# Low parts of the turned probabilities on GpSimd, and the neighbourhood's row tiles turned by VectorE through DRAM

## The chip, the cores and the metric

The kernel runs on one core of a Trainium2 chip. The metric is the device time of one execution in microseconds (us); the median of three runs is taken. The engines are named as the profile names them: PE (TensorE's matmuls), PEld (its weight loads), DVE (VectorE), ACT (ScalarE), POOL (GpSimd) and SP (SyncE, which issues nearly all DMAs).

## The reference

The kernel computes two layers of a hybrid attention block on 16 meta tokens and 512 grid tokens (64 by 8), in float32, and a final normalisation. Of each layer:

```python
h = rms_norm(x, norm_g)
qa, ka, va, za, qb, kb, vb, zb, ga, gb = split_cols(einsum('bld,de->ble', h, w_in))
qa, ka = (apply_axial_rope(rms_norm(t, g), cos, sin) for t, g in ((qa, q_norm_g), (ka, k_norm_g)))
oa = gqa_attention(qa, ka, va) * silu(za)                 # 8 query heads, 2 key heads, all 528 keys
ob = neighbourhood_attention(qb, kb, vb, rpb) * silu(zb)  # 8 heads, a clamped window of 8 x 16 keys, plus the meta keys
mixed = sigmoid(ga) * (oa @ w_o_attn) + sigmoid(gb) * (ob @ w_o_na)
x = x + mixed @ w_out
```

Both attentions are a softmax of scores (the second with a learned bias by relative place) times the values. `gqa_attention` is called the global branch here, `neighbourhood_attention` the neighbourhood.

## The kernel before

Activations lie with features on the partitions and tokens along the row. Every large matmul is made of three: a float32 operand is split into a high part (rounded to the matmul's type, a cast on ACT) and a low part (the rest, a subtraction), and high by high, high by low and low by high are added in PSUM.

**Weights.** A product (`product`, `project`) multiplies a chunk of 128 weight columns by all tokens. Its weights come in two halves of 128x512: a DMA brings `raw`, ACT casts it to `whi` (L240), POOL subtracts to get `wlo` (L241), PE uses both (L325 to L327). `raw`, `whi` and `wlo` have 4 buffers each, and halves are asked for 3 ahead. In the first layer a product runs over two spans of 264 tokens (2 x 24 matmuls), each in one of two PSUM banks; in the second most run over one span of 512. `y` names the products with the two output matrices, which use one half each.

**The two branches** run beside the products. After each span `tick()` is called (in the second layer also in the middle of a span), and `GQA_AT` and `NA_AT` say at which tick after its start a piece of work makes each step. A new unit of the global branch (one head, 256 queries; 16 a layer) and a new head of the neighbourhood (8 a layer) start every fourth tick at most.

A unit of the global branch (`global_unit`): `scores` (PE `S`, DVE maximum L837, ACT exponential L841, giving `P`), `turn` (DVE transposes 32x32 blocks in place, L867, and a DMA writes the tile to DRAM), `back` (four DMAs read it so that blocks land in their turned places, L877), `split_part` (ACT casts `pth`, L193; DVE subtracts `ptl`, L194), `split_ends` (the same for the meta keys, `ga`, L896 and L898) and `sums` (PE `av`, L905). `combine` then copies half of the result on ACT (`cmb`, L769) and adds it on DVE.

A head of the neighbourhood (`windowed_head`): `prepare` loads a bias tile of 128x960, `scores` (PE `Sb`, DVE L990, ACT exponential L992, in place in the bias tile), then nine 128-row transposes on PE into PSUM banks `ta`, `tb`, `tc` (L129) in three steps, each followed by a split from PSUM (`tah`/`tal`, `tbh`/`tbl`, `na`), and `sums` (PE `avb`, L1052), collected at the end of the tick by `combine`. In the first layer there is one more transpose, `tm`, for the meta queries.

**What sets the order.** A scheduler lays the recorded instructions out into one fixed row for each engine. Program order is its guide, `high_priority` (as in `split`) moves instructions ahead, and it also moves instructions of other work forward where it reckons that an engine would stand idle. On the chip each engine goes through its row strictly in order, and waits on semaphores. SP does the same with the DMAs.

Of the kernel before, what the change touches and what calls it, by code (L numbers as in the profile page):

```python
# [11 lines left out]
F32 = mybir.dt.float32  # L12
# [24 lines left out]
GQA_AT = ({"scores": (0, 1), "turn": (1, 2), "back": 3, "split": (5, 5), "ends": 5, "divide": (3, 4, 6), "sums": (7, 7)},  # L37
          {"scores": (0, 1), "turn": (1, 2), "back": 3, "split": (5, 5), "ends": 5, "divide": (3, 4, 6), "sums": (7, 7)})
NA_AT = ({"stages": (0, 2, 5, 5, 5, 7), "values": (3, 4), "divide": (3, 4, 6)},
         {"stages": (0, 2, 4, 5, 5, 7), "values": (3, 4), "divide": (3, 4, 6)})  # L40
# [55 lines left out]
def trunk_kernel(ctx: ExitStack, tc: tile.TileContext, xT, w, gn, gf, bias, rope, out):  # L96
# [94 lines left out]
    def split(hi, lo, src):  # L191
        with tc.high_priority():
            split_at["hi"] = nc.scalar.copy(hi, src)  # L193
            split_at["any"] = nc.vector.tensor_sub(lo, src, hi.bitcast(F32))  # L194
# [259 lines left out]
    for l in range(DEPTH):  # L454
# [310 lines left out]
        def combine(tag, o, hh, av, c0, n):  # L765
# [4 lines left out]
            with ExitStack() as held:  # L770
                if "max" in newest:
                    held.enter_context(tc.issue_after(newest["max"].ins))
                nc.vector.tensor_add(o[r, c0:c0 + n], av[r, :n], t[r, :n])
# [73 lines left out]
        def global_unit(kv, parts, n, name, done):  # L847
# [35 lines left out]
            def split_part(kt):  # L883
                v = c["both"][:, :width * 4].rearrange("p (x k i) -> p x k i", k=4, i=32)[:, :, kt:kt + per]
                th, tl = slot("G", f"pth{name}_{kt}", F32R), slot("G", f"ptl{name}_{kt}", F32R)
                split(*(t[:, :width * per].rearrange("p (k x i) -> p x k i", k=per, i=32) for t in (th, tl)), v)
# [4 lines left out]
            def split_ends():  # L891

                tm, m = pad_tile("ga"), c["meta"][:, :n]
                with tc.high_priority():
                    for t in range(len(parts)):
                        nc.scalar.copy(tm[32 * t:32 * t + 32, n * t:n * (t + 1)], m)  # L896
                    for t in range(len(parts)):
                        nc.vector.tensor_sub(tm[64 + 32 * t:96 + 32 * t, n * t:n * (t + 1)], m, tm[:32, :n].bitcast(F32))  # L898
# [67 lines left out]

        def windowed_head(hd):
# [39 lines left out]
            def transposes1():  # L1007
                pb = c["p"]
                tp = bank(ps_t, f"ta{nm}", "tp")
                for i, (b, o0) in enumerate(((0, 80), (1, 16), (1, 144), (2, 0))):  # L1010
                    transposed(tp[:, P * i:P * (i + 1)], pb[b][:, o0:o0 + P])
                c["a"] = slot("B", f"tah{nm}", F32R), slot("B", f"tal{nm}", F32R)
                split(c["a"][0][:, :512], c["a"][1][:, :512], tp)
                if full:
                    ps = bank(ps_t, f"tm{nm}", "tp")[:32]
                    transposed(ps[:, :P], c["pm"])
                    ps = ps[:, :NMETA]
                    mh = pad_tile("mm")
                    nc.vector.tensor_copy(mh[:32], ps)
                    nc.vector.tensor_sub(mh[64:96], ps, mh[:32].bitcast(F32))  # L1020
                    c["mt"] = mh

            def transposes2():
                pb = c["p"]
                tp = bank(ps_t, f"tb{nm}", "tp")
                transposed(tp[:, 0:P], pb[2][:, P:2 * P])
                transposed(tp[:, P:2 * P], pb[3][:, 0:P])
                transposed(tp[:EDGE, 2 * P:3 * P], pb[0][:, :EDGE])
                transposed(tp[:EDGE, 3 * P:4 * P], pb[3][:, P:P + EDGE])
                c["b"] = bh, bl = slot("B", f"tbh{nm}", F32R), slot("B", f"tbl{nm}", F32R)  # L1030
                split(bh[:, :256], bl[:, :256], tp[:, :256])
                split(bh[:EDGE, 256:512], bl[:EDGE, 256:512], tp[:EDGE, 256:512])

            def transposes3():
                tp = bank(ps_t, f"tc{nm}", "tp")
                transposed(tp[:64, :P], c["bias"][:, BLK_META:BLK_META + 64])

                c["m"] = tm = pad_tile("na")
                split_meta([(tm[:, P:2 * P], tp[:, :P]), (tm[:, :P], tp[:, :P])], inner)

            def sums():
                VB2, o = kvq[j]["v2"], kvq[j]["o"]
                av = bank(ps_a, f"avb{nm}", "avn")
                seq = [(5, c["m"], 0, 128, 384)]
                for t in c["a"]:
                    seq += [(0, t, 0, 0, 256), (1, t, 256, 128, 384)]
# [268 lines left out]
```

## Time and profile before

| | us |
|---|---|
| three runs: median (lowest, highest) | 853.73 (852.26, 855.82) |
| the profiled execution, its own time | 855.46 |
| its span, first to last instruction | 853.1 |
| PE busy in it (share) | 825.1 (97%) |
| DVE, ACT, POOL busy | 552.0, 473.7, 382.6 |
| mean granted TensorE clock | 0.992 |

Busy time is the union of an engine's instructions in the profile. A matmul's duration there runs from its start to the end of its results, and the next one starts before that; how long PE takes for one is read from start to start. "Idle before" an instruction is time in which its engine did nothing, and the name behind it is the instruction whose end released it.

### The profile page before, as it was taken

How to read it: one execution, taken by the hardware profiler on the slowest of the kernel's cores; microseconds unless marked ns; L12 is line 12 of the kernel's file. 1: busy time of each engine (PE TensorE's matmuls, PEld its weight loads, DVE VectorE, ACT ScalarE, POOL GpSimd, SP SyncE). 2: the span in 40 equal slices, each digit the busy share in tenths (PEclk: the TensorE clock that was granted, in tenths of full speed). 3: DMA queues.
4: the chain of work that ended last, by engine and by line, in shares of the span. 5: the costliest groups of instructions: out<-in, count | busy, mean ns of one | idle time of the engine just before them, and what ended most of it. 6: DMA issues, size and time to landing. Idle time of an engine off the chain costs nothing.

```text
span 853.1 us, 16107 instructions
## 1 busy us (share of the span) xinstructions
PE 825.1 (97%) x5662; PEld 762.1 (89%) x5662; DVE 552.0 (65%) x1218; ACT 473.7 (56%) x1137; POOL 382.6 (45%) x296
## 2 busy tenths in 40 slices
PE   9999899989999999899999999999999999999997
PEld 9999899989999999899998989898987778878786
DVE  7976658777776675436447657777777657555633
ACT  8654677566764555333435456576757645543422
POOL 1663343343343333545765554443534433445851
PEclk9999999999999999999999999999999999999999
DMA  7277464566544564334555575657476655544502
GB/s 275 90 194 215 122 183 122 172 205 169 169 139 137 164 184 145 112 100 144 147 143 130 142 212 161 170 165 238 124 206 172 193 163 169 169 151 145 176 13 99
DMA packets 113249, 135.00 MB, mean 158 GB/s; under 512 B 31888, under 2 KB 66192, under 8 KB 113168
## 3 DMA queue, kind: packets, MB, share of 16 engines
q1 hardware_dynamic: 112448, 132.90, 53.0%
q8 instruction: 45, 0.74, 0.4%
q10 hardware_dynamic: 720, 1.06, 0.3%
q14 instruction: 36, 0.29, 0.1%
HBM read 98.50 MB, written 21.84 MB: 141 GB/s over the span
## 4 chain that ended last, share of the span: by engine, by line
PE 78%; DVE 8%; ACT 6%; issue 4%; DMA 2%; SPq 1%; POOL 1%; POOLq 0%; ACTq 0%; DVEq 0%
PE pp L327 16%; PE pp L325 16%; PE pp L326 16%; PE av L905 4%; PE y L327 3%; PE y L326 3%; PE y L325 3%; PE avb L1052 2%; DVE ptl L194 2%; PE pf L1234 2%; PE pf L1236 2%; PE pf L1235 2%; PE S L556 2%; PE S L557 1%; DVE ga L898 1%
## 5 line engine op out<-in xcount | busy, mean ns | idle before, releaser
L241 POOL TENSOR_TENSOR wlo<-raw,whi 128x512 fp32r<-128x512 f32 x210 | 289.2, 1386 | 404.7 <-ACT whi L240 325.0
L325 PE MATMUL pp<-hh,whi 128*128 128x264 f32 (+3 forms) x1040 | 326.6, 314 | 2.7 <-DVE mg L1131 1.5
L327 PE MATMUL pp<-hh,wlo 128*128 128x264 f32 (+3 forms) x1040 | 326.2, 314 | 1.3 <-POOL wlo L241 1.2
L326 PE MATMUL pp<-hl,whi 128*128 128x264 f32 (+3 forms) x1040 | 324.3, 312 | 0.0
L327 PEld LDWEIGHTS pp<-hh,wlo 128*128 128x128 f32 x1040 | 196.8, 189 | 12.9 <-POOL wlo L241 2.1
L325 PEld LDWEIGHTS pp<-hh,whi 128*128 128x128 f32 x1040 | 196.5, 189 | 12.4 <-DVE mg L1131 1.7
L326 PEld LDWEIGHTS pp<-hl,whi 128*128 128x128 f32 x1040 | 197.0, 189 | 9.5
L240 ACT CAST whi<-raw 128x512 fp32r<-128x512 f32 x210 | 127.6, 618 | 109.1 <-PE pp L326 41.1
L867 DVE STREAM_TRANSPOSE P<-P 128x512 f32<-128x512 f32 x64 | 46.4, 727 | 36.4 <-ACT P L841 35.7
L194 DVE TENSOR_TENSOR ptl<-P,pth 128x512 fp32r<-128x512 f32 x64 | 53.8, 841 | 5.4 <-ACT pth L193 4.7
L837 DVE CUSTOM_DVE_ANT_1 P<-S,r 128x528 f32<-128x528 f32 x64 | 44.9, 701 | 16.0 <-PE S L557 15.1
L1131 DVE TENSOR_TENSOR mg<-pp,rbc 128x264 f32<-128x264 f32 (+1 forms) x48 | 24.8, 517 | 39.0 <-PE pp L327 38.5
L841 ACT ACTIVATE P<-P,st 128x528 f32<-128x528 f32 x64 | 47.2, 737 | 1.9
L1132 ACT ACTIVATE mg<-mg 128x264 f32<-128x264 f32 (+1 forms) x48 | 23.7, 494 | 35.0 <-DVE mg L1131 34.8
L992 ACT ACTIVATE bias<-bias,stb 128x208 f32<-128x208 f32 (+1 forms) x64 | 31.0, 486 | 20.0 <-DVE stb L990 19.9
L193 ACT CAST pth<-P 128x512 fp32r<-128x512 f32 x64 | 39.3, 614 | 0.1
L840 ACT ACTIVATE st<-st 128x1 f32<-128x1 f32 x64 | 13.0, 203 | 45.4 <-DVE st L837 44.6
L905 PE MATMUL av<-ptl,VA 128*128 128x256 f32 x128 | 34.1, 294 | 3.3 <-DVE ptl L194 3.1
L326 PE MATMUL pp<-mx,whi 128*128 128x264 f32 x128 | 36.6, 286 | 0.0
L327 PE MATMUL pp<-mx,wlo 128*128 128x264 f32 x128 | 36.4, 284 | 0.0
L325 PE MATMUL pp<-mx,whi 128*128 128x264 f32 x128 | 36.3, 284 | 0.0
L905 PE MATMUL av<-pth,VA 128*128 128x256 f32 x128 | 34.8, 295 | 0.0
(534 smaller groups left out, 1731.6 us busy)
## 6 DMA issues: line engine op xcount, KB each, us to landing
raw<-in_w_dram SPq DMA_DIRECT2D x210, 256.0 KB
turn<-P SPq DMA_DIRECT2D x32, 528.0 KB
P<-turn SPq DMA_DIRECT2D x128, 128.0 KB
bias<-in_bias_dram SPq DMA_DIRECT2D x16, 480.0 KB
KB<-KB SPq DMA_DIRECT2D x24, 272.0 KB
rawl<-in_w_dram SPq DMA_DIRECT2D x16, 256.0 KB
x<-in_xT_dram SPq DMA_DIRECT2D x8, 264.0 KB
xr<-in_xT_dram SPq DMA_DIRECT2D x8, 264.0 KB
```

The source lines that it names most:

```text
L193: split_at["hi"] = nc.scalar.copy(hi, src)
L194: split_at["any"] = nc.vector.tensor_sub(lo, src, hi.bitcast(F32))
L240: cast = nc.scalar.copy(hi, raw)
L241: sub = nc.gpsimd.tensor_sub(lo, raw, hi.bitcast(F32))
L325: nc.tensor.matmul(ps, wh, rh[:, a:b], start=i == 0, stop=False)
L326: nc.tensor.matmul(ps, wh, rl[:, a:b], start=False, stop=False)
L327: nc.tensor.matmul(ps, wl, rh[:, a:b], start=False, stop=i == n - 1)
L837: newest["max"] = nc.vector.tensor_tensor_reduce(p[:n].rearrange("p (i k) -> p i k", i=2), S[:n, :, :HALF], scale[:n].unsqueeze(2).to_broa ...
L841: nc.scalar.activation(p[:n], p[:n], AF.Exp, bias=st[:n, 1:2], scale=1.0, accum_out=st[:n, 2:3] if total is None else total)
L867: nc.vector.transpose(c["both"][:n, a:b], c["both"][:n, a:b])
L905: nc.tensor.matmul(c["av"], rows2(c["t"][i][0]), c["t"][i][1], start=i == 0, stop=i == 8)
L992: nc.scalar.activation(pb[b], pb[b], AF.Exp, bias=st[:, b:b + 1], scale=-1.0, accum_out=total[:, b:b + 1])
```

## The change

The diff, cut to its core (names in the code before stand above):

```diff
-GQA_AT = (... "divide": (3, 4, 6) ...          # both layers
+GQA_AT = (... "divide": (2, 3, 5) ...
-NA_AT = ({"stages": (0, 2, 5, 5, 5, 7), ...}, {"stages": (0, 2, 4, 5, 5, 7), ...})
+NA_AT = ({"stages": (0, 2, 3, 4, 4, 4, 6, 7), ...}, {"stages": (0, 2, 3, 4, 4, 6, 7), ...})

-    def split(hi, lo, src):
+    def split(hi, lo, src, eng=nc.vector):
...
-            split_at["any"] = nc.vector.tensor_sub(lo, src, hi.bitcast(F32))
+            split_at["any"] = eng.tensor_sub(lo, src, hi.bitcast(F32))

             def split_part(kt):
...
-                split(*(... for t in (th, tl)), v)
+                split(*(... for t in (th, tl)), v, nc.gpsimd)
             def split_ends():
...
-                        nc.vector.tensor_sub(tm[64 + 32 * t:96 + 32 * t, ...], m, tm[:32, :n].bitcast(F32))
+                        nc.gpsimd.tensor_sub(tm[64 + 32 * t:96 + 32 * t, ...], m, tm[:32, :n].bitcast(F32))

-            def transposes1(): ...   # 4 PE transposes, split of 128x512 from PSUM
-            def transposes2(): ...   # 4 PE transposes, splits of 128x256 and 80x256 from PSUM
-            def transposes3(): ...   # 1 PE transpose, split of the meta keys
+            def turn():
+                v = c["bias"][:, EDGE:EDGE + 832].rearrange("p (s x) -> p s x", s=2)[:, :, :3 * P]
+                for s in range(2):
+                    nc.vector.transpose(v[:, s], v[:, s])
+                c["there"] = dpool.tile([P, 6 * P], F32, tag="turnedb", bufs=3, name=f"turnb{nm}")
+                nc.sync.dma_start(c["there"].rearrange("p (s x) -> p s x", s=2), v)
+            def meta_turn(): ...     # first layer: tm and its split, as before
+            def edges():
+                pb = c["p"]
+                tp = bank(ps_t, f"tb{nm}", "tp")
+                transposed(tp[:EDGE, :P], pb[0][:, :EDGE])
+                transposed(tp[:EDGE, P:2 * P], pb[3][:, P:P + EDGE])
+                transposed(tp[:64, 2 * P:3 * P], c["bias"][:, BLK_META:BLK_META + 64])
+                ...                  # splits of 80x256 and of the meta keys
+            def back():
+                there = c["there"].rearrange("(b j) (s x) -> j s b x", j=32, s=6)
+                for q in range(4):
+                    nc.sync.dma_start(c["bias"][32 * q:32 * q + 32, :6 * P].rearrange("j (s b i) -> j s b i", s=6, b=4),
+                                      there[:, :, :, 32 * q:32 * q + 32])
+            def split_tiles():
+                v = c["bias"][:, :6 * P].rearrange("p (s t x) -> p t s x", s=2, t=3)
+                c["a"] = slot("B", f"tah{nm}", F32R), slot("B", f"tal{nm}", F32R)
+                split(*(... for t in c["a"]), v[:, :2])      # 128x512, from SBUF
+                split(*(... for t in c["b"]), v[:, 2])       # 128x256, from SBUF
```

So three of a head's nine transposes stay on PE (two of 80 columns, one of 64, all in one bank), and the six whole tiles of 128x128 take the way of the global branch: two DVE transposes of 128x384 in place, one DMA out, four DMAs back with pieces of 32 numbers, and a split from SBUF at tick 6. `sums` makes the same eleven matmuls in another order (meta keys, edges, whole tiles), writing the tiles in queries' blocks, and `combine` reads them with the columns rearranged. In the global branch the subtractions `ptl` and `ga` move from DVE to POOL, and the steps that spread the inverse sums come one tick earlier.

How the rows change is shown at two places. In names, the numbers are layer, then chunk or head (and unit), then half, then a serial number: `whi0_16_1` is the cast of the second weight half of chunk 16 in layer 0, `avb0_1` the products of the neighbourhood's head 1.

**First place: layer 0, chunk 16, beside head 1.** On ACT, before:

```order
L240 CAST whi0_16_0_1822<-raw0_16_0_1695 128x512
L240 CAST whi0_16_1_1828<-raw0_16_1_1820 128x512
L193 CAST tah0_1_1789<-ta0_1_1784 128x512
L757 ACTIVATE zb0_1t_1688<-zb0_1_1687 128x264
L193 CAST tbh0_1_1802<-tb0_1_1797 128x256
L792 ACTIVATE na0_122<-tc0_1_1808,inner_130 32x128 x2
L193 CAST tbh0_1_1802<-tb0_1_1797 80x256
```

and now:

```order
L769 COPY cmb1973_1974<-avb0_1_1937 64x512
L769 COPY cmb1977_1978<-avbm0_1_1949 64x16
L996 ACTIVATE bias0_2_1763,sumb0_1_1762<-bias0_2_1763,stb0_2_1861 128x208
L996 ACTIVATE bias0_2_1763,sumb0_1_1762<-bias0_2_1763,stb0_2_1861 128x272 x2
L996 ACTIVATE bias0_2_1763,sumb0_1_1762<-bias0_2_1763,stb0_2_1861 128x208
L240 CAST whi0_16_1_1822<-raw0_16_1_1814 128x512
L240 CAST whi0_12_0_1989<-raw0_12_0_1820 128x512
```

The cast of the second half stood right behind that of the first, ahead of head 1's split; now it stands behind the copy of head 1's products and four exponentials of head 2. On PE, before, the product's two halves followed each other:

```order
L326 MATMUL pp0_16_0_1995<-hl0_3_179,whi0_16_0_1822 128x264
L327 MATMUL pp0_16_0_1995<-hh0_3_178,wlo0_16_0_1823 128x264
L325 MATMUL pp0_16_0_1995<-hh0_4_190,whi0_16_1_1828 128x264
L326 MATMUL pp0_16_0_1995<-hl0_4_191,whi0_16_1_1828 128x264
L327 MATMUL pp0_16_0_1995<-hh0_4_190,wlo0_16_1_1829 128x264
L325 MATMUL pp0_16_0_1995<-hh0_5_203,whi0_16_1_1828 128x264
L326 MATMUL pp0_16_0_1995<-hl0_5_204,whi0_16_1_1828 128x264
```

and now, right behind the last product of head 1:

```order
L129 MATMUL tm0_2_2026<-ident_100,pm0_126 32x128
L556 MATMUL S0_1_1_0_1964<-KA0h0_931,Q20_0_578 128x264
L557 MATMUL S0_1_1_0_1964<-KA0l0_932,Q20_0_578 128x264
L556 MATMUL S0_1_1_0_1964<-KA0h0_931,Q20_0_578 128x264
L557 MATMUL S0_1_1_0_1964<-KA0l0_932,Q20_0_578 128x264
L129 MATMUL tb0_2_2030<-ident_100,bias0_2_1763 80x128 x2
L325 MATMUL pp0_16_0_1999<-hh0_4_190,whi0_16_1_1822 128x264
L326 MATMUL pp0_16_0_1999<-hl0_4_191,whi0_16_1_1822 128x264
L556 MATMUL S0_1_1_1_2067<-KA0h0_931,Q20_0_578 128x264
L557 MATMUL S0_1_1_1_2067<-KA0l0_932,Q20_0_578 128x264
L556 MATMUL S0_1_1_1_2067<-KA0h0_931,Q20_0_578 128x264
L327 MATMUL pp0_16_0_1999<-hh0_4_190,wlo0_16_1_1823 128x264
```

The first half of chunk 16 has been multiplied for both spans ahead of these rows, and the second half comes behind head 1's products, scores of the global branch and head 2's edges.

**Second place: layer 1, chunk 39 and unit 0 of head 5 of the global branch.** On POOL, before (`za` is a gate):

```order
L241 TENSOR_TENSOR wlo1_40_0_9489<-raw1_40_0_9480,whi1_40_0_9488 128x512
L241 TENSOR_TENSOR wlo1_40_1_9554<-raw1_40_1_9486,whi1_40_1_9553 128x512
L241 TENSOR_TENSOR wlo1_47_1_9589<-raw1_47_1_9551,whi1_47_1_9588 128x512
L822 TENSOR_TENSOR za1_2_8236<-za1_2_8236,sumsa1_2_9571 128x512
L241 TENSOR_TENSOR wlo1_41_0_9595<-raw1_41_0_9586,whi1_41_0_9594 128x512
```

and now:

```order
L241 TENSOR_TENSOR wlo1_40_0_9489<-raw1_40_0_9480,whi1_40_0_9488 128x512
L241 TENSOR_TENSOR wlo1_40_1_9557<-raw1_40_1_9486,whi1_40_1_9556 128x512
L241 TENSOR_TENSOR wlo1_47_1_9589<-raw1_47_1_9554,whi1_47_1_9588 128x512
L194 TENSOR_TENSOR ptl1_5_0_0_9458<-P1_5_0_9296,pth1_5_0_0_9457 128x8x2x32
L898 TENSOR_TENSOR ga0_120<-pm1_5_0_9410,ga0_120 32x128 x2
L194 TENSOR_TENSOR ptl1_5_0_2_9462<-P1_5_0_9296,pth1_5_0_2_9461 128x8x2x32
L241 TENSOR_TENSOR wlo1_41_0_9595<-raw1_41_0_9586,whi1_41_0_9594 128x512
```

The unit's three subtractions stand between the low parts of the weights; before, DVE had them, in this row:

```order
L1131 TENSOR_TENSOR mg1_34_5_9479<-pp1_39_0_9492,rbc1_6350 128x512
L194 TENSOR_TENSOR ptl1_5_0_0_9458<-P1_5_0_9296,pth1_5_0_0_9457 128x8x2x32
L898 TENSOR_TENSOR ga0_120<-pm1_5_0_9410,ga0_120 32x128
L194 TENSOR_TENSOR ptl1_5_0_2_9462<-P1_5_0_9296,pth1_5_0_2_9461 128x8x2x32
L898 TENSOR_TENSOR ga0_120<-pm1_5_0_9410,ga0_120 32x128
L773 TENSOR_TENSOR oa1_2_9205<-av1_5_0_9522,cmb9532_9533 64x256
```

On PE the unit's products stand among those of `y`, which follow the end of chunk 39 (its last cast weights are `whi1_39_1`, whose buffer `whi1_47_1` takes over). The rows from the first product of the unit to the first that uses its last `ptl`, before:

```order
L905 MATMUL av1_5_0_9522<-pth1_5_0_0_9457,VA21_6772 128x256
L327 MATMUL y01_47_0_9557<-ob1_1_8346,wlo1_47_0_9483 128x512
L325 MATMUL y01_47_0_9557<-ob1_2_8826,whi1_47_0_9482 128x512
L326 MATMUL y01_47_0_9557<-ob1_2_8826,whi1_47_0_9482 128x512
L905 MATMUL av1_5_0_9522<-ptl1_5_0_0_9458,VA21_6772 128x256
L905 MATMUL av1_5_0_9522<-pth1_5_0_0_9457,VA21_6772 128x256
L905 MATMUL av1_5_0_9522<-ptl1_5_0_0_9458,VA21_6772 128x256
L905 MATMUL av1_5_0_9522<-pth1_5_0_2_9461,VA21_6772 128x256
L327 MATMUL y01_47_0_9557<-ob1_2_8826,wlo1_47_0_9483 128x512
L905 MATMUL av1_5_0_9522<-ptl1_5_0_2_9462,VA21_6772 128x256
```

and now:

```order
L325 MATMUL y01_47_0_9560<-ob1_2_8829,whi1_47_0_9482 128x512
L905 MATMUL av1_5_0_9530<-pth1_5_0_0_9457,VA21_6772 128x256
L326 MATMUL y01_47_0_9560<-ob1_2_8829,whi1_47_0_9482 128x512
L905 MATMUL av1_5_0_9530<-ptl1_5_0_0_9458,VA21_6772 128x256
L905 MATMUL av1_5_0_9530<-pth1_5_0_0_9457,VA21_6772 128x256
L905 MATMUL av1_5_0_9530<-ptl1_5_0_0_9458,VA21_6772 128x256
L905 MATMUL av1_5_0_9530<-pth1_5_0_2_9461,VA21_6772 128x256
L327 MATMUL y01_47_0_9560<-ob1_2_8829,wlo1_47_0_9483 128x512
L325 MATMUL y01_47_0_9560<-ob1_3_9266,whi1_47_0_9482 128x512
L905 MATMUL av1_5_0_9530<-ptl1_5_0_2_9462,VA21_6772 128x256
```

The last of these rows stands 16 places behind the last product with `whi1_39_1` before, and 17 places now: the distance on PE is nearly the same, while what must be done within it has moved from DVE's row into POOL's.

76 lines of the change are left out of this document (34 added, 42 removed).

## The prediction

> **What bounds the kernel now.** I read the page's head first, then its chain of waits, then the list of PE's waits (total us, count, longest).
>
> ```profile
> span 853.1 us, 16107 instructions
> PE 825.1 (97%) x5662; PEld 762.1 (89%) x5662; DVE 552.0 (65%) x1218; ACT 473.7 (56%) x1137; POOL 382.6 (45%) x296
> PE 78%; DVE 8%; ACT 6%; issue 4%; DMA 2%; SPq 1%; POOL 1%; POOLq 0%; ACTq 0%; DVEq 0%
> PE tb L129 <- DVE mm L1020: 3.3, 2, 3.0
> PE av L905 <- DVE ptl L194: 3.1, 5, 1.0
> PE y L325 <- DVE mg L1131: 2.5, 1, 2.5
> PE tc L129 <- DVE mm L1020: 2.0, 1, 2.0
> PE tb L129 <- DVE tal L194: 1.5, 2, 1.0
> PE pp L327 <- POOL wlo L241: 1.2, 2, 0.7
> PE pp L325 <- ACT whi L240: 1.1, 1, 1.1
> ```
>
> PE is the bound: it stands for 853.1 - 825.1 = 28.0 us, in single waits of at most 3 us. So a change pays by what it takes from PE, and costs by what it makes PE wait; what it does to the sum of DVE or POOL counts only through such waits. The load of 45% on POOL says nothing of how late one of its results may come.
>
> What PE needs for one instruction is read from start to start in the timeline (start, duration):
>
> ```profile
> 152.41 0.29 PE L327 MATMUL pp<-hh,wlo 128*128 128x264 f32 x1
> 152.53 0.60 PE L129 MATMUL ta<-ident,bias 128*128 128x128 f32 x4
> 152.97 0.27 PE L129 MATMUL tm<-ident,pm 128*32 128x128 f32 x1
> 560.55 0.28 PE L905 MATMUL av<-pth,VA 128*128 128x256 f32 x1
> 560.67 0.28 PE L905 MATMUL av<-ptl,VA 128*128 128x256 f32 x1
> 562.07 0.39 PE L325 MATMUL pp<-hh,whi 128*128 128x512 f32 x1
> 562.30 0.39 PE L326 MATMUL pp<-hl,whi 128*128 128x512 f32 x1
> ```
>
> A product of 264 columns takes 0.12 us (152.41 to 152.53), one of 256 also 0.12, one of 512 0.23, a transpose of 128 columns (152.97 - 152.53) / 4 = 0.11. One half of a weight chunk lasts 24 x 0.12 = 2.9 us on PE in the first layer.
>
> One place shows what a late weight does, in the second layer (the last brackets: idle before, and the releaser):
>
> ```profile
> 642.46 0.62 ACT L240 CAST whi<-raw 128x512 fp32r<-128x512 f32 x1
> 643.13 0.50 PE L325 MATMUL pp<-hh,whi 128*128 128x512 f32 x1 [1.08 <-ACT whi L240]
> 643.21 2.99 POOL L241 TENSOR_TENSOR wlo<-raw,whi 128x512 fp32r<-128x512 f32 x2 [8.64 <-ACT whi L240]
> 643.63 1.42 DVE L194 TENSOR_TENSOR ptl<-P,pth 128x512 fp32r<-128x512 f32 x1 [0.48 <-ACT pth L193]
> 644.55 0.50 PE L327 MATMUL pp<-hh,wlo 128*128 128x512 f32 x1 [0.52 <-POOL wlo L241]
> ```
>
> The cast came late on ACT, PE stood 1.08 us for it, and 0.52 us again for the low part behind it. POOL had stood 8.64 us before: an idle engine does not help when its input is late.
>
> The prices (busy us, mean ns of one; then, for two of them, the shortest, median and longest):
>
> ```profile
> L241 POOL TENSOR_TENSOR wlo<-raw,whi 128x512 fp32r<-128x512 f32 x210 | 289.2, 1386 | 404.7 <-ACT whi L240 325.0 <-PE ta L129 14.1 <-PE tc L129 9.6
> L240 ACT CAST whi<-raw 128x512 fp32r<-128x512 f32 x210 | 127.6, 618 | 109.1 <-PE pp L326 41.1 <-issue 19.7 <-PE y L326 17.8
> L325 PE MATMUL pp<-hh,whi 128*128 128x264 f32 x752 | 216.3, 288 | 0.0
> L194 DVE TENSOR_TENSOR ptl<-P,pth 128x512 fp32r<-128x512 f32 x64 | 53.8, 841 | 5.4 <-ACT pth L193 4.7
> L898 DVE TENSOR_TENSOR ga<-pm,ga 32x128 fp32r<-32x128 f32 x64 | 32.0, 499 | 2.3 <-DMA raw<-in_w_dram 0.7
> L193 ACT CAST pth<-P 128x512 fp32r<-128x512 f32 x64 | 39.3, 614 | 0.1
> L769 ACT COPY cmb<-avb 64x512 f32<-64x512 f32 x16 | 9.3, 580 | 7.2 <-PE avb L1052 7.0
> L769 ACT COPY cmb<-avbm 64x16 f32<-64x16 f32 x8 | 1.3, 165 | 0.0
> L992 ACT ACTIVATE bias<-bias,stb 128x272 f32<-128x272 f32 x32 | 16.3, 510 | 0.0
> L992 ACT ACTIVATE bias<-bias,stb 128x208 f32<-128x208 f32 x32 | 14.8, 462 | 20.0 <-DVE stb L990 19.9
> L992 ACT ACTIVATION_READ_ACCUMULATOR bias<-bias,stb 128x1 f32 x64 | 12.0, 187 | 0.0
> L867 DVE STREAM_TRANSPOSE P<-P 128x512 f32<-128x512 f32 x32 | 22.7, 710 | 17.4 <-ACT P L841 17.1
> L573 POOL COPY qmt<-q 128x16 f32<-128x16 f32 x4 | 2.1, 532 | 3.8 <-DVE q L502 3.8
> L194 DVE TENSOR_TENSOR ptl<-P,pth x64: 649/692/1776, 79.3 to 758.7; 128x512 fp32r<-128x512 f32 x64
> L241 POOL TENSOR_TENSOR wlo<-raw,whi x210: 1253/1296/2194, 19.5 to 791.7; 128x512 fp32r<-128x512 f32 x105
> SPq L877 <- DMA turn<-P: 28.4, 23, 3.6
> ```
>
> **What goes from PE.** Six of a head's nine transposes, for 16 heads: 96 x 0.11 = 10.5 us. PE is the bound, so they count in full. The eleven products of a head keep their sizes.
>
> **What moves between engines.** DVE loses 64 `ptl` (53.8 us) and `ga` (32.0) and gets 32 transposes of 128x384, by the row of 128x512 0.710 x 384 / 512 = 0.53 each, 17 us: some 483 us. POOL gets 64 `ptl` at the price of `wlo` (same operation and size), 1.386 each, 88.7 us, and the `ga`. No row shows POOL subtracting 32x128: by size from `wlo` it would be 0.35, its small copy `qmt` takes 0.53; I take 0.42, since the operation is that of `wlo`: 64 x 0.42 = 27 us. POOL comes to about 498 us of 853, still no bound by its sum.
>
> **What stands in other rows.** Here lies the cost. The scheduler's new rows put a second half's cast behind the copy of a head's products, and the `ptl` of a unit between low parts of weights. Each engine works through its row, so PE's products, ACT, POOL and PE again form a loop; if the loop's work on the other engines is longer than PE's own between its two ends, PE stands for the difference.
>
> First place. From the last product of head 1 the loop is: its end behind its slot 0.288 - 0.122 = 0.17; `cmb` 0.580 and `avbm`'s 0.165; the four exponentials 2 x (0.462 + 0.187) + 2 x (0.510 + 0.187) = 2.69; `whi` 0.618; `wlo` 1.386: 5.6 us. PE has between them nine products of 0.122 and three transposes, about 1.4. It stands for 4.2 us. Before, the cast stood ahead of the head's split and was there in time. Behind the waiting cast stand that of the next chunk and so the next `wlo`: the loop delays the weights ahead too.
>
> Second place. `whi1_47_1` takes the buffer of `whi1_39_1`, so it starts when PE has used that: 0.17, then `whi` 0.618, `wlo` 1.386, `ptl` 1.386, two `ga` 0.84, `ptl` 1.386 until PE's product with the last `ptl`: 5.8 us. PE has between them 11 products of 0.231 and 5 of 0.118: 3.1. It stands 2.7 us. Before, DVE's own row (two `ptl` of 0.841 and a `ga`) beside two casts of 0.614 took 3.0, just covered.
>
> I followed such loops for all of PE's instructions, in the order of the rows of both kernels, with the mean durations of the groups above, of loops that overlap the best set alone, and no DMA in them. Before they give 43.8 us in 42 places, where the trace shows 28.0 (0.64 of it). With usual instead of mean durations (`wlo` 1.30, its median) they give 21.0 in 27 places (the trace is 1.33 of that). Now, with means: 143.2 us in 65 places. Of these, products of the global branch behind `ptl` have 51.7 (27 places; before 3.2), weights behind a head's products 31.0 (8), other weights 24.0 (12; all weights before 6.0), heads behind the split of the whole tiles 11.2 (6), scores and output products behind late parts 12.2 (4), others 13.1 (8). With usual durations: 119.7 in 63. The difference is 143.2 - 43.8 = 99.4, or 119.7 - 21.0 = 98.7: I take 99. Its ends, by the two ratios to the trace, are 0.64 x 99 = 64 and 1.33 x 99 = 131.
>
> **What I cost at nothing.** The DMAs: 16 more out and 64 more back, all on SP. The global branch's way back is asked for two ticks ahead of its split; the neighbourhood's now as well (4 and 6). SP's longest wait for a tile that is not yet there is 3.6 us in the rows above, and the weights behind it are asked for three halves, 8.6 us, ahead; if that cover is gone, each of 16 heads may cost 3.6. No DMA was a releaser of PE above 1 us. The sums that are spread a tick earlier: no wait of PE above 1 us was for them. The rearranged copies of `combine`: the same sizes. The split from SBUF for one from PSUM: the same size, between 0.65 (the shortest `ptl`) and 0.84 a tile on DVE, and late `tal` are among the loops.
>
> A slower pair of engines is in the sum already: 643.63 shows a `ptl` on DVE of 1.42 us beside a busy POOL, the usual one being 0.692, and the means hold such cases on either engine (1776 of 692, 2194 of 1296). [...]
>
> **The sum.** 853.1 - 10.5 + 99 = 941.6 for the span. The profiled execution (855.46) lies 1.7 above the median, 853.73, so the time is 853.7 - 10.5 + 99 = 942. Its own range is 853.7 - 10.5 + 64 = 907 to 853.7 - 10.5 + 131 = 974.
>
> **The rivals.**
> *Only the global branch bites.* The weights are cast in time because the queues settle otherwise than the rows suggest (what PE waits for once shifts all behind it), and only `ptl` on POOL is late: 853.7 - 10.5 + 51.7 - 3.2 = 892. For it: with PE already late, the second loop at one place may find its inputs there. Against it: 31.0 us lie behind the copies of products, which start only when PE is done. Chance 0.11.
> *SP holds the weights up.* Each head's way back waits in SP's queue for its way out, and costs PE the longest such wait, 16 x 3.6 = 58 us on top: 1000. Against it: 23 waits of this kind now have no reply on PE. Chance 0.08. [...]
> *Faster.* The loops don't close: POOL stood idle for more than half of its span, and takes the new work in those gaps, so PE keeps its 10.5 us and loses also the waits for `mm` and `tal` ahead of transposes, 3.3 + 2.0 + 1.5 = 6.8: 836. It decides if the new standing is under 15 us, a sixth of what the rows give. Against it: the first place alone gives 4 us, with every link of the loop in a row that is fixed. Chance 0.04.
> *No change*, with loops that happen to give back the 10.5 and the 6.8: 0.03.
>
> **How the numbers follow.** The forecast, slower by loops of both kinds, has 0.74. Differences under 0.5% are about what a measurement of this kernel can tell from none; all slower cases together have 0.93, within it 0.03, faster 0.04. The range reaches down past the first rival, to 885, and up to 990, short of the second's 1000.
>
> **What the profile after would show.** PE busy about 815, in a span of 942: idle near 127 us. PE's 5662 instructions become 5566. Its list of waits is headed by POOL's `wlo`, POOL's `ptl` and ACT's `whi`, with tens of us each, in single waits of 2 to 5 us; DVE near 483, POOL near 498. ACT waits for the products of heads as it does now, but the weights' cast stands behind. I am wrong if PE's waits name a DMA, if `ptl` on POOL takes far from 1.39, or if PE's idle time stays under 50 us.

## The result, and the profile after

The changed kernel takes 972.91 us (971.51 to 975.33), beside 854.12 of the kernel before: 1.139 times as long (95% interval 1.136 to 1.143), or 119 us more. Forecast were 942, within 885 to 990. The page's head, its row of PE's granted clock in 40 slices, and PE's list of waits (total us, count, longest):

```profile
span 973.6 us, 16185 instructions
PE 874.7 (90%) x5566; PEld 791.2 (81%) x5566; DVE 497.2 (51%) x1118; ACT 476.0 (49%) x1137; POOL 496.4 (51%) x428
PEclk9999997899779999799999999988898989999999
PE av L905 <- POOL ptl L194: 33.7, 36, 1.7
PE pp L325 <- ACT whi L240: 20.9, 12, 6.6
PE pp L327 <- POOL wlo L241: 9.4, 16, 0.9
PE pp L325 <- DVE mg L1149: 4.0, 1, 4.0
PE tm L129 <- DVE VB L194: 3.8, 3, 1.5
PE avb L1069 <- ACT tah L193: 2.9, 4, 0.9
```

PE has 96 instructions fewer, and yet is busy 50 us longer (825.1 before), and idle 98.9 us where it was 28.0. The waits are those that the two places stand for: `ptl` on POOL, the weights' cast on ACT, and the low part behind it. The longer busy time comes with a lower granted clock: 0.936 on the mean, where it was 0.992. From 650 to 750 us PE was busy for 97.94 us at a clock of 1.00 before, and for 78.38 us at 0.86 after (the columns are the length, the busy time of PE, PEld, DVE, ACT and POOL, then PE's granted clock, the DMA share and GB/s):

```profile
650.00:750.00 100.00, 97.94 (x500) 81.45 (x499) 65.54 (x128) 58.85 (x140) 41.66 (x32) 1.00 0.55 169
```

```profile
650.00:750.00 100.00, 78.38 (x403) 65.90 (x403) 49.47 (x120) 47.85 (x121) 45.10 (x39) 0.86 0.53 151
```

The first place, chunk 16 beside head 1, in the timeline after (start, duration; the last brackets: idle before, and the releaser):

```profile
128.51 0.28 PE L1069 MATMUL avb<-tbl,VB 128*128 128x256 f32 x1
128.82 0.48 ACT L193 CAST VB<-vtb 128x384 fp32r<-128x384 f32 x1 [0.42 <-PE avb L1069]
129.33 0.58 ACT L769 COPY cmb<-avb 64x512 f32<-64x512 f32 x1
129.95 0.28 PE L129 MATMUL tm<-ident,pm 128*32 128x128 f32 x1 [1.16 <-DVE VB L194]
130.22 0.47 ACT L996 ACTIVATE bias<-bias,stb 128x208 f32<-128x208 f32 x1 [0.24 <-DVE stb L994]
131.25 0.39 PE L556 MATMUL S<-KA0h,Q 128*128 128x264 f32 x1 [1.02 <-DVE stb L994]
132.05 0.19 ACT L996 ACTIVATION_READ_ACCUMULATOR bias<-bias,stb 128x1 f32 x1
132.15 1.12 ACT L240 CAST whi<-raw 128x512 fp32r<-128x512 f32 x2
132.82 4.25 POOL L241 TENSOR_TENSOR wlo<-raw,whi 128x512 fp32r<-128x512 f32 x3 [5.91 <-ACT whi L240]
134.17 0.59 PE L327 MATMUL pp<-hh,wlo 128*128 128x264 f32 x1
134.99 0.28 PE L327 MATMUL pp<-hh,wlo 128*128 128x264 f32 x1
135.11 0.28 PE L325 MATMUL pp<-hh,whi 128*128 128x264 f32 x1
```

From head 1's last product (128.51) to the first with the late `wlo` (134.17) pass 5.66 us. PE has 1.4 us of its own work between, so the loop costs 4.2 us, as was worked out. The parts are not all those that were worked out, so the equal sum is in part luck: from 130.22 to the cast at 132.15 the four exponentials take 1.9 us and not 2.7, while the cast of `VB` (0.48) and a wait for `stb` (0.24) stand in ACT's row too. POOL had stood idle for 5.91 us before its subtraction. Nor is it the weights that PE stands for here: it stands 1.16 and 1.02 us for `VB` and `stb`, both made by DVE, the rest of the 4.2 us lies in longer slots, and the late `wlo` comes at about the time when PE gets to it. Without these waits PE would have stood for `whi` and `wlo` instead, since the chain over ACT and POOL takes as long. Around 134 us:

```profile
133.00:135.00 2.00, 2.00 (x9) 1.79 (x10) 1.94 (x6) 1.71 (x5) 2.00 (x2) 0.51 0.06 22
135.00:138.00 3.00, 3.00 (x27) 3.00 (x27) 2.86 (x7) 1.72 (x5) 2.07 (x2) 1.00 1.03 351
```

In the first stretch 9 instructions take 2 us at a granted clock of 0.51, in the second 27 take 3 us at 1.00: about 0.22 and 0.11 us each. The second place:

```profile
807.82 0.62 ACT L240 CAST whi<-raw 128x512 fp32r<-128x512 f32 x1 [2.14 <-DMA turn<-P]
808.51 1.30 POOL L241 TENSOR_TENSOR wlo<-raw,whi 128x512 fp32r<-128x512 f32 x1 [1.46 <-DMA therea<-inva]
809.77 1.28 POOL L194 TENSOR_TENSOR ptl<-P,pth 128x512 fp32r<-128x512 f32 x1
811.11 0.38 PE L905 MATMUL av<-ptl,VA 128*128 128x256 f32 x1 [1.17 <-POOL ptl L194]
811.13 0.97 POOL L898 TENSOR_TENSOR ga<-pm,ga 32x128 fp32r<-32x128 f32 x2
812.18 1.26 POOL L194 TENSOR_TENSOR ptl<-P,pth 128x512 fp32r<-128x512 f32 x1
813.50 0.39 PE L905 MATMUL av<-ptl,VA 128*128 128x256 f32 x1 [1.19 <-POOL ptl L194]
```

PE stands twice, 1.17 + 1.19 = 2.4 us for 2.7 worked out: cast, low part, `ptl`, two `ga` and `ptl` follow each other with no gap above 0.1 us. The profile puts the cast's wait down to a DMA; PE's last product with the buffer that the cast takes over ended at 807.74, so the cast could not have come much sooner.

**What PE's time is made of.** From start to start of PE's instructions, against the usual slots (0.122 for 264 columns and so on): what one gap is longer by more than 0.4 us is counted as standing, what a slot is longer by otherwise, where it is over 1.4 times the usual, as slow slots.

| | standing, us (places) | slow slots, us | granted clock |
|---|---|---|---|
| before | 23.4 (19) | 24.1 | 0.992 |
| after | 108.2 (94) | 66.7 | 0.936 |

So 84.8 us more of standing, 42.6 us more of slow slots and 10.5 us less of transposes: 117 of the 120.5 us between the spans. The slow slots grew where the granted clock was at half (some 4 us before, some 48 after); the others stayed near 20 us.

### The profile page after: what moved, and what is told of

It reads as the page before. It is cut to its first block, busy times and chain, and to the rows that moved or that the text cites. A ratio compares the mean times of both kernels' runs of the same rounds, so it can differ in the third digit from the quotient of the medians.

```text
span 973.6 us, 16185 instructions
## 1 busy us (share of the span) xinstructions
PE 874.7 (90%) x5566; PEld 791.2 (81%) x5566; DVE 497.2 (51%) x1118; ACT 476.0 (49%) x1137; POOL 496.4 (51%) x428
## 3 DMA queue, kind: packets, MB, share of 16 engines
q1 hardware_dynamic: 166976, 145.49, 51.7%
q10 hardware_dynamic: 720, 1.06, 0.3%
## 5 line engine op out<-in xcount | busy, mean ns | idle before, releaser
L325 PE MATMUL pp<-hh,whi 128*128 128x264 f32 (+3 forms) x1040 | 343.6, 331 | 24.9 <-ACT whi L240 20.9
L327 PE MATMUL pp<-hh,wlo 128*128 128x264 f32 (+3 forms) x1040 | 341.1, 330 | 9.6 <-POOL wlo L241 9.4
L326 PE MATMUL pp<-hl,whi 128*128 128x264 f32 (+3 forms) x1040 | 338.2, 325 | 0.0
L325 PEld LDWEIGHTS pp<-hh,whi 128*128 128x128 f32 x1040 | 210.5, 202 | 38.2 <-ACT whi L240 24.3
L327 PEld LDWEIGHTS pp<-hh,wlo 128*128 128x128 f32 x1040 | 208.9, 202 | 27.6 <-POOL wlo L241 16.2
L326 PEld LDWEIGHTS pp<-hl,whi 128*128 128x128 f32 x1040 | 210.4, 202 | 10.1
L194 POOL TENSOR_TENSOR ptl<-P,pth 128x512 fp32r<-128x512 f32 x64 | 85.0, 1333 | 109.0 <-ACT pth L193 81.4
L905 PE MATMUL av<-ptl,VA 128*128 128x256 f32 x128 | 38.1, 320 | 33.8 <-POOL ptl L194 33.7
L905 PEld LDWEIGHTS av<-ptl,VA 128*128 128x128 f32 x128 | 24.3, 190 | 43.1 <-POOL ptl L194 42.8
L773 DVE TENSOR_TENSOR oa<-av,cmb 64x256 f32<-64x256 f32 x32 | 13.4, 420 | 82.3 <-ACT cmb L769 82.2
L898 POOL TENSOR_TENSOR ga<-pm,ga 32x128 fp32r<-32x128 f32 x64 | 29.4, 459 | 24.2 <-ACT ga L896 15.3
```

Of the source, the lines that this page charges most:

```text
L194: split_at["any"] = eng.tensor_sub(lo, src, hi.bitcast(F32))
L325: nc.tensor.matmul(ps, wh, rh[:, a:b], start=i == 0, stop=False)
L326: nc.tensor.matmul(ps, wh, rl[:, a:b], start=False, stop=False)
L327: nc.tensor.matmul(ps, wl, rh[:, a:b], start=False, stop=i == n - 1)
L905: nc.tensor.matmul(c["av"], rows2(c["t"][i][0]), c["t"][i][1], start=i == 0, stop=i == 8)
```

## The experiments

Two theories besides that of the rows were tried: that POOL is too slow for what it was given ("GpSimd theory"), and that the neighbourhood's DMAs are what costs ("DMA theory"). For each kernel the loops were added up in its new rows as in the prediction, before it ran; the factor of 1.30 is 119.2 + 10.5 us of the change by its 99.4 us more of loops.

**E1, the neighbourhood's part alone.**

```diff
-split(*(... for t in (th, tl)), v, nc.gpsimd)          # of the changed kernel
+split(*(... for t in (th, tl)), v)
-nc.gpsimd.tensor_sub(tm[64 + 32 * t:...                # ga
+nc.vector.tensor_sub(tm[64 + 32 * t:...
-GQA_AT ... "divide": (2, 3, 5)
+GQA_AT ... "divide": (3, 4, 6)
```

> The neighbourhood's part of the change alone: its whole tiles turned by VectorE through DRAM; ptl and ga stay on VectorE, the inverse sums keep their ticks. Rows theory (PE waits in loops that the new rows make; each us of loop costs 1.30 us, since after the change 99.4 us more of loops cost 119.2 + 10.5 us): loops 109.4 us against 43.8 before, so 65.6 x 1.30 - 10.5 = +75, about 929 us, and PE's waits are headed by whi. GpSimd theory (what costs is that ptl and ga are dearer on GpSimd): with them on VectorE only the 10.5 us of transposes are left, 843 us, or 870 if the new splits from SBUF collide with GpSimd. DMA theory (the tiles land late, or their DMAs take bandwidth from the weights): as the rows theory here, some 915 to 930, but with DMAs named as releasers of tens of us.

Measured: 930.37 us, ratio 1.0876 (1.0852 to 1.090). The rows theory said 929. POOL does no more here than before (378.3 us busy), so the 74 us are not its work. The 870 of the GpSimd theory holds the author's estimate of 27 us at most for the 32 new splits, each longer by the mean of `ptl` on DVE (0.84). The DMA theory had 915 to 930, with DMAs named as releasers of tens of us, so the number alone doesn't part it from the rows theory; PE's list of waits, which names no DMA, does:

```profile
PE pp L325 <- ACT whi L240: 22.0, 12, 6.8
PE pp L327 <- POOL wlo L241: 8.2, 16, 0.8
PE av L905 <- ACT pth L193: 5.5, 3, 4.4
```

One step further back there is a DMA. In three places, 13.0 of the 22.0 us for `whi`, ACT had last waited for the weights' DMA. At the longest (6.8 us) SP had stood 12.9 us in its row for DVE's `tbl`, and issued the weights after that. The loops of the prediction have no DMA in them.

**E2, the global branch's part alone**: the three edits of E1 made to the kernel before, the other way round.

> The global branch's part alone: ptl and ga on GpSimd, the inverse sums a tick earlier, the neighbourhood as before. Rows theory: loops 57.2 us against 43.8 before, 13.4 x 1.30 = +17, about 871 us. GpSimd theory: here lies most of the loss, 892 us (the 51.7 us of loops over ptl of the changed kernel, without the 10.5 us of transposes, so 902) or more. DMA theory: no change, 854 us.

Measured: 875.64 us, ratio 1.0235 (1.0216 to 1.0253), 20 us more; the rows theory said 871, the GpSimd theory 892 or more. PE waits 20.1 us for `ptl` on POOL (26 times) in place of 33.7 (36 times) with the whole change. The parts alone give 74.5 + 19.7 = 94 of the 119 us; together they make longer loops than apart (99.4 us for 65.6 + 13.4).

**E3, the small subtractions alone.**

```diff
-nc.vector.tensor_sub(tm[64 + 32 * t:...                # ga, of the kernel before
+nc.gpsimd.tensor_sub(tm[64 + 32 * t:...
```

> The smallest part alone: only the 64 (and 4) small subtractions ga on GpSimd, all else as before. Rows theory: loops 28.9 us against 43.8 before, the loops over ga on VectorE go; the trace of before stood 29.2 us at its 43.8 us of loops (0.67), so -10 us, 844 us; -19 us and 835 by the factor of 1.30. GpSimd theory: an operation that takes as long on GpSimd (0.46 us) as on VectorE (0.50) in a queue with longer ones ahead gains nothing: 854 us or slower. DMA theory: 854 us.

Measured: 842.38 us, ratio 0.9846 (0.983 to 0.9862): faster than both kernels by a part of the change that made it slower (842.55 is the longest of its five runs, 853.63 the shortest of nine of the kernel before). The instruction is dearer on POOL (0.638 us on the mean here; on DVE before 0.499, and usually 0.284). What went is its place in DVE's row, ahead of what PE waits for: on PE's list the waits for `mm` fall from 5.3 to 0.8 us, those for `ga` from 1.0 to none. Standing is 15.9 us and slow slots 18.7, together 12.9 us less than before, for 13.5 us measured.

**E4, the neighbourhood's DMAs on POOL's queue** (edit of E1):

```diff
-nc.sync.dma_start(c["there"]..., v)         # out, and the four back alike
+nc.gpsimd.dma_start(c["there"]..., v)
```

> As the neighbourhood's part alone, but its 80 DMAs are issued from GpSimd's queue instead of SyncE's: the same bytes and pieces, the same steps and ticks. With them out of SyncE's row, the scheduler no longer puts the weights' second halves behind a head's copy. Rows theory: loops 73.9 us against 43.8, 30.1 x 1.30 - 10.5 = +29, about 883 us, some 46 us under the neighbourhood's part alone (plus what issuing 80 DMAs costs GpSimd). DMA theory: bytes and pieces are the same, so as the neighbourhood's part alone within some 10 us. GpSimd theory: GpSimd gets more to do, so slower than the neighbourhood's part alone.

Measured: 915.28 us, ratio 1.0686 (1.0657 to 1.0715): 15 us less than E1, where the rows theory expected some 46. The waits that it meant to take away went, and others came. PE's list, and POOL's time to issue the way back:

```profile
PE avb L1069 <- ACT tah L193: 13.6, 8, 3.7
PE avb L1069 <- DVE tal L194: 6.9, 7, 1.5
PE avb L1069 <- DVE tbl L194: 5.9, 7, 1.8
PE pp L327 <- POOL wlo L241: 2.9, 5, 1.5
L1045 POOL DMA_DIRECT2D bias<-turnb x64 | 55.1, 1057 | 39.5 <-PE tb L129 13.7 <-PE S L557 9.5 <-PE pp L327 6.1
```

The weights' waits fell from 22.0 + 8.2 us to 1.7 for `whi` and 2.9 for `wlo`, so these DMAs in SP's row had put the weights back. But on POOL the 64 issues of the way back take 55.1 us in the row of `wlo` (1.06 us each, overlapping), and PE now waits 26.4 us for the heads' splits. DVE, with the same work as in E1, is busy 589.5 us in place of 562.7; its `ptl` take 0.982 us in place of 0.816. The loops had left out both, and how much of the miss each carries was not separated. In size the DMA theory (within some 10 us of E1) came nearer here than the rows theory. Its premise of the same pieces does not hold on the way, though: the 12.59 MB go in 4864 packets from POOL's queue; on SP's they took 54528 (its queue has 166976 in E1, 112448 here).

**E5, weights asked for earlier** (edit of E1):

```diff
-for l_, c_, i in order[len(loaded):n + 1]:     # the DMAs of raw
+for l_, c_, i in order[len(loaded):n + 2]:
```

> As the neighbourhood's part alone (930.4 us), but the DMA of each weight half is written one half earlier in the program (raw keeps its 4 buffers): nothing is added, only rows change. Rows theory: the new rows have loops of 143.3 us against 109.4 in the neighbourhood's part alone and 43.8 before: 99.5 x 1.30 - 10.5 = +119, about 975 us. DMA theory (weights come late behind the neighbourhood's DMAs): asking earlier helps or does nothing, 930 us or less. GpSimd theory: nothing moves to GpSimd, 930 us.

Measured: 971.13 us, ratio 1.1374 (1.134 to 1.1407): 41 us slower than E1 by an edit that adds no instruction. The rows theory said 975, both others 930 or less. PE waits 33.2 us for `whi`, up to 9.2 at once; there the weights' DMA came after 18.5 us that SP stood for DVE's `tbl`, as in E1.

**E6, the way back in wide pieces** (edit of the changed kernel):

```diff
-nc.sync.dma_start(c["bias"][32 * q:32 * q + 32, :6 * P].rearrange("j (s b i) -> j s b i", s=6, b=4),
-                  there[:, :, :, 32 * q:32 * q + 32])
+nc.sync.dma_start(c["bias"][32 * q:32 * q + 32, :6 * P], c["there"][32 * q:32 * q + 32])
```

> The whole change, with the neighbourhood's way back in pieces of 3072 B (rows as they lie in DRAM, so the blocks come back unturned and the output isn't the reference's) in place of 128 B: the same bytes, 4 DMAs a head as before. The scheduler reckons with the pieces, so the rows move too: loops of 116.0 us in place of 143.2. Rows theory: (116.0 - 43.8) x 1.30 - 10.5 = +83, about 939 us. DMA theory (the small pieces cost the time): the 31 us of weights behind heads and the 11 us behind the tiles go in full with their slow clock, 920 us or less. GpSimd theory: nothing changes on GpSimd, 973 us.

Measured: 940.29 us, ratio 1.1002 (1.0973 to 1.1031); expected by the rows 939, by the DMAs 920 or less. It saves 33 us; the moved rows, 27.2 us of loops less, account for 35. The pieces and the rows change together here, so their shares rest on that sum alone. On PE's list the waits for `ptl`, `whi` and `wlo` stay (32.6, 21.0 and 8.7 us); those for heads' splits fall from 7.0 to 2.6, for the scores' inputs from 4.7 to 1.0, and that for `VB` (3.8) goes. In the changed kernel the DMA share can be read too: its SP queue holds 145.49 MB on 51.7% of 16 engines' span, beside 132.90 MB on 53.0% before, so 503 against 452 us; the 12.6 MB more cost 4.07 us per MB where the rest costs 3.40. By an estimate from these two, with the way out at the price of the rest, the way back in 128 B costs 1.4 times that. With the wide pieces the same 145.49 MB take 51.8% of E6's span, 486 us, so some 17 less. It is small beside the span, and no wait of PE is for it; one of ACT is (0.7 us, ahead of `tah`), and one of POOL (3.3 us).

**E7, the large subtractions alone.**

```diff
-split(*(... for t in (th, tl)), v)                     # of the kernel before
+split(*(... for t in (th, tl)), v, nc.gpsimd)
```

> As before, but the 64 ptl on GpSimd (1.33 us there, 0.84 on VectorE); ga stays on VectorE and the inverse sums keep their ticks. Rows theory: loops 39.8 us against 43.8 before, -4.0 x 0.9 to 1.3 = -4 to -5, 851 us: no dearer than before, though each ptl takes longer. GpSimd theory: it is the ptl that cost, 64 x 0.49 = 31 us, of which the larger part shows: 871 to 887 us. DMA theory: 856 us.

Measured: 855.42 us, ratio 1.001 (0.9994 to 1.0027): no difference. The rows theory said 4 to 5 us less than before (851), so it was 5 to 6 us off and the gain that it forecast is not there; the GpSimd theory said 871 to 887. PE waits 8.0 us for `ptl`, 15 times. One thing no theory named: `ga`, which stays on DVE here, takes 0.892 us on the mean, where it took 0.499 before (below, under DVE beside POOL).

**E10, the global branch without the earlier inverse sums**: E2 with `"divide": (3, 4, 6)`.

> The global branch's part without its third piece: ptl and ga on GpSimd, the inverse sums at their old ticks (3, 4, 6). ptl alone costs nothing and ga alone gains, the whole part costs 20 us. Rows theory: loops 51.9 us against 57.2 with the earlier sums and 43.8 before: 8.1 x 1.3 to 1.5 = +10 to +12, 865 us. Rival, that the earlier inverse sums (whose products are GpSimd's) carry the loss: the sum of the parts alone, 842 + 1 = 843 us.

Measured: 864.21 us, ratio 1.0111 (1.0079 to 1.0143), as the rows theory said (865). So the earlier inverse sums cost 11 us of E2, and the pair of `ptl` and `ga` on POOL 9, where each alone costs nothing or gains: both stand in one row between the same two ends on PE, as at the second place. PE's wait for `ptl` grows from 8.0 us in E7 to 17.2.

**E8, how long PE must stand for its clock to fall.**

```diff
+for n, (m, k) in enumerate(plan):             # in place of the whole computation
+    for i in range(m):
+        nc.tensor.matmul(ps, wt, rhs, start=i == 0, stop=i == m - 1)
+    ...                                       # a copy on DVE, k more, a cast on ACT that makes the next rhs
```

> Not the reference's computation: bursts of 100 products of 264 columns, between which TensorE waits for a VectorE copy, 0 to 12 more copies and an ACT copy (each length three times), then groups of short bursts of 4 to 24 products with such waits between them; the output is zeros. Clock theory (standing lowers the clock that is granted to TensorE, and the next products take 0.22 in place of 0.12 us): a single wait of about 1 us is followed by no slow product, longer ones or several in a row by some 15 to 30 slow ones, 2 to 3 us more each time. Rival: the slow products in the changed kernel come from late operands or from weight loads; then every burst here runs at 0.12 us from its first or second product on, whatever the wait.

Between bursts of 100 products, PE stood (beyond a usual slot) for 1.1 to 5.3 us. Up to 2.0 us, in 10 cases, only the first product took 0.22 us. At 2.27 us two of three cases, at 2.60 two of three, and from 3.26 us on all nine were followed by 13 to 27 products of 0.22 us, 1.4 to 2.8 us more. Four stretches of 3 us, two behind a standing of 1.92 and 2.60 us, and two of 2.27 and 3.26 (PE's granted clock is the third number from the end):

```profile
143.20:146.20 3.00, 3.00 (x24) 3.00 (x25) 0.00 (x0) 0.00 (x0) 0.00 (x0) 1.00 0.00 0
157.70:160.70 3.00, 3.00 (x18) 3.00 (x19) 0.00 (x0) 0.00 (x0) 0.00 (x0) 0.71 0.02 5
204.80:207.80 3.00, 3.00 (x25) 3.00 (x26) 0.00 (x0) 0.00 (x0) 0.00 (x0) 1.00 0.00 0
253.10:256.10 3.00, 3.00 (x19) 3.00 (x20) 0.00 (x0) 0.00 (x0) 0.00 (x0) 0.74 0.00 0
```

Several short ones do the same: bursts of 8 products (1.0 us) with a standing of 1.2 to 1.3 us between them ran at a mean clock of 0.62 with the burst behind them, bursts of 12 (1.5 us) with 1.6 to 1.9 us between did not slow:

```profile
436.00:448.00 12.00, 8.64 (x39) 7.82 (x40) 1.30 (x3) 1.43 (x4) 0.00 (x0) 0.62 0.00 0
487.00:500.00 13.00, 8.27 (x61) 7.63 (x62) 2.19 (x6) 1.27 (x4) 0.00 (x0) 1.00 0.00 1
```

The rival, late operands or weight loads, falls: the operands here are the same for a whole burst. What decides between the groups can be read from the clock itself. In this run it changes 32 times, always at a whole multiple of 3.413 us from the other changes, wherever a standing began. When the run is cut into stretches of 3.413 us at these times, the full clock fell behind each stretch in which PE was busy for 0.46 of it or less, and behind none with 0.50 or more. Two standings of 2.27 us, the first inside one stretch, the second across two:

```profile
155.54:158.96 3.41, 1.30 (x11) 1.26 (x11) 1.33 (x4) 0.41 (x1) 0.00 (x0) 1.00 0.00 0
158.96:162.37 3.41, 3.41 (x18) 3.41 (x17) 0.00 (x0) 0.00 (x0) 0.00 (x0) 0.50 0.02 5
169.20:172.61 3.41, 2.50 (x21) 2.29 (x19) 0.74 (x3) 0.00 (x0) 0.00 (x0) 1.00 0.00 0
172.61:176.03 3.41, 2.21 (x18) 2.22 (x19) 0.59 (x2) 0.41 (x1) 0.00 (x0) 1.00 0.00 0
176.03:179.44 3.41, 3.41 (x30) 3.41 (x30) 0.00 (x0) 0.00 (x0) 0.00 (x0) 1.00 0.02 5
```

So in this run the clock went with PE's busy share of such a stretch, and not with the length of one standing. In the changed kernel the changes also lie whole multiples of 3.413 us apart; there the two groups of stretches overlap, between 0.53 and 0.63.

**E9, a version that beats both**: E3 with two ticks changed.

```diff
-GQA_AT ... "sums": (7, 7)
+GQA_AT ... "sums": (7, 8)
-NA_AT = ({"stages": (0, 2, 5, 5, 5, 7)        # first layer
+NA_AT = ({"stages": (0, 2, 4, 5, 5, 7)
```

> A version that should beat both: as before, with only ga on GpSimd, the products of a unit's second pair of tiles one tick later (8 for 7) and the first layer's first transposes one tick earlier (4 for 5). Rows theory: loops 23.3 us against 43.8 before and 28.9 with ga alone: by what ga alone paid (13.5 us for 14.9 us of loops, 0.91), -20.5 x 0.91 = -19, 836 us. GpSimd and DMA theories: the ticks change nothing, 842 us as with ga alone.

Measured: 839.15 us, ratio 0.9817 (0.9788 to 0.9847). It beats both kernels; against E3 the intervals overlap, so the two ticks by themselves are not shown to help.

| | loops over those before, us | measured over before, us | without 10.5 of transposes, us |
|---|---|---|---|
| E9 | -20.5 | -16.0 | |
| E3 | -14.9 | -13.5 | |
| E7 | -4.0 | +1.2 | |
| E10 | +8.1 | +9.1 | |
| E2 | +13.4 | +19.7 | |
| E4 | +30.1 | +59.4 | +69.9 |
| E1 | +65.6 | +74.5 | +85.0 |
| E6 | +72.2 | +86.1 | +96.6 |
| after | +99.4 | +118.8 | +129.3 |
| E5 | +99.5 | +116.9 | +127.4 |

Each difference is to the median of before on the same chip, in the same set of runs. Two kernels with nearly equal loops, the whole change and E5, cost the same, though one of them moves nothing to POOL. E4 leaves the line, with the issues and the longer DVE instructions that its loops don't hold. The price of a us of loops, by the last filled column, is 0.8 to 1.5 us in eight kernels and 2.3 in E4; in E7 the few us have the wrong sign. The 1.30 was taken from the changed kernel's own time, so that row is no test of it.

## Why the prediction was right, point by point

*PE is the bound and pays only by standing*: right, with one thing left out (below). *96 transposes less*: 5566 instructions, as said. *DVE 483 and POOL 498*: 497.2 and 496.4; the transposes took 0.562 us (0.53 said), `ptl` on POOL 1.333 (1.386), `ga` 0.459 (0.42). Neither sum had a say: E5 costs as much as the whole change with POOL at 379.0.

*The loops*: the 65 places that were picked had 143.2 us by the rows. From one end of each loop to the other, less PE's usual slots between, the trace after shows 131 at these same places, and the trace of before 29 at its 42 for 43.8, so 102 more for 99 said; the other 25 of the 127 us lie outside these places. The two places worked out by hand gave 4.2 us for 4.2, though with other parts and other waits than those named, and 2.4 for 2.7.

*The step that was off* is the sum's 99, taken for all that the loops cost: it was 127. Standing grew by 84.8 us, and by 42.6 the slots behind it, at half the granted clock, for which the prediction had no term; the list of before showed its waits as few and short, and the trace of before, at a mean clock of 0.992, has only three stretches of 3.4 us at half the clock, ahead of its end, to price it from. The standing by itself came out below the 99. So PE's busy time was 875 and not 815, and its idle time 98.9 and not 127. The time came out inside the forecast's own range (907 to 974; 0.64 x 99 is 63, so rather 906) only at its upper end, 131 for the term. That end stood there for another reason, the ratio of the trace to usual durations, so that it was wide enough is luck.

*Which loops*: the three names that head PE's list are those that were given, their sizes not. `ptl` has 33.7 us on PE's list for 51.7 in the loops, `wlo` has 9.4 and not tens, and the single waits for these two are at most 1.7 and 0.9 us, not 2 to 5. The neighbourhood's part is the dearer one (E1 against E2). So the rival "only the global branch bites" had it the wrong way round.

*The DMAs at nothing*: nearly right for this kernel. PE's list names one DMA, with 0.2 us. But at one place SP's row did something like what the second rival said, with the way back of the global branch in place of a head's:

```profile
666.39 2.58 SPq L877 DMA_DIRECT2D P<-turn  x4
669.72 0.85 SPq L235 DMA_DIRECT2D raw<-in_w_dram  x2
671.32 0.62 ACT L896 CAST ga<-pm 32x128 fp32r<-32x128 f32 x2 [4.36 <-DMA pm<-turn]
673.45 0.62 ACT L240 CAST whi<-raw 128x512 fp32r<-128x512 f32 x1 [0.77 <-DMA raw<-in_w_dram]
674.12 0.80 PE L325 MATMUL pp<-hh,whi 128*128 128x512 f32 x1 [6.64 <-ACT whi L240]
```

The weights were issued behind the global branch's way back, ACT waited for the meta keys of the same way back and only then cast the weights, and PE stood 6.64 us. That is the longest wait of the run, once, and not the 16 x 3.6 of the rival; the place was among the loops with 3.3 us. In E1 and E5 the longest waits came by SP's row as well, so the row of DMAs belongs among the links of such a loop.

*DVE beside POOL*: what the prediction held only in its means, a `ptl` of 1.42 us on DVE beside a busy POOL where 0.692 is usual, shows in other instructions too. The split of a head's third tiles on DVE, from SBUF, in the changed kernel, and then in E1, where POOL has no `ptl`:

```profile
L194 DVE TENSOR_TENSOR tbl<-bias,tbh 128x256 fp32r<-128x256 f32 x16 | 15.3, 957 | 0.0
```

```profile
L194 DVE TENSOR_TENSOR tbl<-bias,tbh 128x256 fp32r<-128x256 f32 x16 | 7.7, 483 | 0.0
```

The same instruction is twice as long on the mean beside the busier POOL (496.4 us, in E1 378.3). In the changed kernel eight of the sixteen took 0.41 to 0.42 us, with POOL at work for at most 0.34 us of that, and eight took 1.48 to 1.51 us, with POOL at work for at least 1.21 us of it. `tal` goes from 698 to 826 ns. Together that is 16 x (0.474 + 0.128) = 9.6 us of DVE, some of it in loops, for the 27 that the author's estimate had at most. It shows most in E7, where `ga` stays on DVE beside `ptl` on POOL (shortest, median and longest, ns):

```profile
L898 DVE TENSOR_TENSOR ga<-pm,ga x64: 282/1226/1407, 80.1 to 761.2; 32x128 fp32r<-32x128 f32 x64
```

Before, the median was 284. With `ga` on POOL as well (E10) it takes 0.468 us on the mean.

*The faster side* was not for the whole change, but for its smallest piece: `ga` alone on POOL gives 13.5 us, near the 17 that the rival had for loops that don't close.

Left open: why the scheduler puts the weights back behind the neighbourhood's way back. E4 shows that this DMA in SP's row decides it. Its pieces don't, since in E6 the waits for `whi` and `wlo` stay. The scheduler's reckoning was not looked into.

## What to carry to other kernels

Where a bound engine lives on short waits, cost a change by the closed loops of work that it makes in the rows that result, from end to end on that engine, and not by the sums of the other engines: here loops added up before the runs put ten kernels in the order of their times (two pairs of them too near to part). What a us of loops costs had to be measured first, and two sizes were missed: in one the issues of DMAs had been left out, in the other a gain of 4 us did not come. Take a change apart before dropping it: the smallest piece of this one was worth 1.5%, while the piece that it was made for, transposes off PE, cost eight times what it saved (85 us for 10.5). And price standing by more than its length: in E8, 13 to 27 products at half the clock, 1.4 to 2.8 us more, came behind two of three standings of 2.27 us and behind all nine of 3.26 us or more.

## What was not expected of the hardware

In E8 two of three standings of PE of 2.27 us were followed by 13 to 27 products at half the granted clock, and bursts of 8 products with standings of 1.2 to 1.3 us between them ran at a mean clock of 0.62; in the changed kernel slow slots added 42.6 us to 84.8 us of standing. What counted in E8 was whether PE was busy for less than about half of a stretch of 3.413 us (the full clock fell behind 0.46 or less, and stayed behind 0.50 or more), by a grid that the standing did not move. A subtraction of 32x128 on DVE took 1.23 us in the median in place of 0.28 beside POOL's larger subtractions (E7). And 64 DMAs with 128-byte pieces issued from POOL took 55.1 us of POOL's row (E4); on SP an issue took 0.66 us in the median of the changed kernel, in the row that the weights' DMAs need.
